# Chunk states of an SSD scan from three fp32r products of split operands, in place of one fp32 product

## The chip, the cores and the metric

The kernel is one program on one core of a Trainium2 chip. The metric is the device time of one execution in microseconds (us). Three executions of the kernel before took 2356.79, 2356.94 and 2358.75 us; the median is 2356.94 us. TensorE is called PE in the profile, VectorE DVE, ScalarE ACT, GpSimd POOL and SyncE SP.

## The reference

The reference is one layer of a hybrid encoder on 1024 tokens of width 1024: windowed attention beside a Mamba-2 style SSD scan, a merge, a cross-attention and an MLP. The change touches one line of the SSD scan, the state that each chunk of 128 tokens contributes:

```python
xdt = (x * dt[..., None]).reshape(b, c, CHUNK, G, r, P)
decay_states = jnp.exp(a_cs[..., -1:] - a_cs)
states = jnp.einsum('bcsgn,bcgrs,bcsgrp->bcgrpn', Bc, decay_states, xdt)
```

There are 8 groups (G), in each 4 heads of width 64 and a state of 128; 8 chunks; and two directions, forward and backward. So for each group and chunk a matrix B of 128 tokens by 128 state entries is multiplied with x, scaled by a coefficient of its token, head and direction: 128 tokens by 512 columns (two directions of 256). Chunk 0 needs only its forward half and chunk 7 only its backward half.

## The kernel before

All large products are made on PE with operands of the type fp32r. An operand is split into a high part (an ACT copy into an fp32r tile) and a low part (the fp32 value minus the high part, on POOL for weights, on DVE for activations), and three products are summed in PSUM: high by high, high by low, low by high. The helper `mm3` (its products stand at L85, L89 and L90) does this. Smaller products of the scan are single fp32 products.

The scan is `ssd_phase`. Eight groups go through it one after another. For a group four projections run as jobs (`conv_job` 0 and 1 make the two x tiles `cx`, 2 makes B as `cB`, 3 makes C as `cC`), then a `z_job`, whose products `zp` run while the states are computed. A job's weights are loaded one job ahead by `wload`: DMA into `raw`, ACT copy to `whi` (L66), POOL subtraction to `wlo` (L69). `conv_post` follows each conv job: one ACT operation (L379), four DVE operations from PSUM (L383, L385, twice each), an ACT tanh (L387) and a DVE operation (L388).

PE's order is that of the code (`manual_schedule`), and the table `jobs` sets after how many steps of a job another piece runs: in the z job `tm_b` after step 4, `state(q, c)` after step 8c + 8. The other engines' orders are made by a scheduler when the program is built; each engine then takes its instructions strictly in that order.

- `tm_b` turns B to token order: four PE transposes (L482) into one PSUM tile `tm`, an ACT copy (L483) into `btok`, twice.
- `state` scales x on DVE into `xs` (L502, 128x512, both directions always), makes one fp32 product of `btok` and `xs` into the PSUM tile `st` (L506) and adds the result to the running states `prev` (L509 to L514).
- `tm_x`, in job 3, turns the two `cx` tiles into `xtok`; after that the two `cx` buffers are free until the next group's job 0.
- `step` and `prep` make the outputs of a chunk; POOL's `p` (L572, x times the skip weight) belongs to `step`, and runs early since it needs only `xtok`.

The buffers that matter: `xs` has 2, `cx` has 2, the PSUM tag `p` (`tm`, `zp`, `st` and others) has 4.

Of the kernel before, what the change touches and what calls it, by code (L numbers as in the profile page):

```python
# [7 lines left out]
F32 = mybir.dt.float32  # L8
F32R = mybir.dt.float32r
I32 = mybir.dt.int32  # L10
AF = mybir.ActivationFunctionType
ALU = mybir.AluOpType
# [4 lines left out]
P = 128  # L17
S = 1024
D = 1024
NT = 8  # L20
# [395 lines left out]
def ssd_phase(kx, ins, dr):  # L416
# [3 lines left out]
    V, A, G, PE = nc.vector, nc.scalar, nc.gpsimd, nc.tensor  # L420
    with tc.tile_pool(name="p1", bufs=1) as sp, tc.manual_schedule(engines={mybir.EngineType.PE}):
        ca = kx.conv_pool
# [3 lines left out]
        def heads(ap):  # L426
            return ap.rearrange("p (h q) -> p h q", h=4)
# [46 lines left out]
                    V.scalar_tensor_tensor(zb, zb, 1.0, zp, ALU.add, ALU.mult)  # L474
            return load, run

        def tok_major(src, dst):
            for b in range(2):
                pt = kx.pp.tile([P, 512], F32, tag="p", name="tm")
                for j in range(4):  # L480
                    c = 4 * b + j
                    PE.transpose(pt[:, j * P:(j + 1) * P], src[:, c * P:(c + 1) * P], kx.ident)  # L482
                A.activation(dst[:, 4 * b:4 * b + 4], pt.rearrange("p (c j) -> p c j", c=4), AF.Copy)  # L483

        def tm_x(q):
            q.xtok = ca.tile([P, NT, 256], F32, tag="xtok", bufs=1, name="xtok")
            for i in range(2):
                tok_major(q.cx[i], q.xtok[:, :, i * P:(i + 1) * P])

        def tm_b(q):  # L490
            q.btok = ca.tile([P, NT, P], F32, tag="btok", bufs=1, name="btok")
            tok_major(q.BT, q.btok)
            q.prev = sp.tile([P, NT, 2, 256], F32, tag="prev", bufs=1, name="prev")

        def decay(q, d, c):
            o = 64 * d + 32 * (c // 4) + 4 * q.g
            return kx.dec[:, o:o + 4, c % 4:c % 4 + 1].broadcast_to([P, 4, 64])

        def state(q, c):
            prev = q.prev  # L500
            xs = sp.tile([P, 2, 4, 64], F32, tag="xs", bufs=2, name="xs")
            V.tensor_tensor(xs, heads(q.xtok[:, c]).unsqueeze(1).broadcast_to([P, 2, 4, 64]),  # L502
                            kx.coef[:, c // 4, c % 4, :, q.hs].unsqueeze(3).broadcast_to([P, 2, 4, 64]), ALU.mult)
            lo, hi = (256 if c == NT - 1 else 0), (256 if c == 0 else 512)
            st = kx.pp.tile([P, 512], F32, tag="p", name="st")
            PE.matmul(st[:, lo:hi], q.btok[:, c], xs.rearrange("p d h q -> p (d h q)")[:, lo:hi],  # L506
                      start=True, stop=True)
            if c == 0:
                A.activation(prev[:, 1, 0], st[:, :256], AF.Copy)  # L509
            elif c < NT - 1:  # L510
                V.tensor_tensor(heads(prev[:, c + 1, 0]), heads(prev[:, c, 0]), decay(q, 0, c), ALU.mult)
                V.tensor_tensor(prev[:, c + 1, 0], prev[:, c + 1, 0], st[:, :256], ALU.add)
            if c > 0:
                A.activation(prev[:, c - 1, 1], st[:, 256:], AF.Copy)  # L514
# [89 lines left out]
        for g in range(NG):  # L604
            q, o = gs[g], gs[g - 1]
            scan = lambda *cs: [(step, o, c) for c in cs] if g else []
            if g == 0:
                job(conv_job(q, 3), {8: [(tm_x, q)]})
            else:
                job(conv_job(q, 0), {8: [(step, o, 7)], 16: [(step, o, 6)]})  # L610
                job(conv_job(q, 1), {8: [(step, o, 5)], 16: [(step, o, 4)]})
                job(gate_job(g), {8: [(step, o, 3)], 16: [(step, o, 2)]})
                job(conv_job(q, 2), {8: [(step, o, 1)], 16: [(yt, o), (step, o, 0)]})
                job(conv_job(q, 3), {8: [(tm_x, q)], 16: [(yt, o)]})
            at = {8 * c + 8: [(state, q, c)] for c in range(NT)}
            at[4] = [(tm_b, q)]
            at[56] += [(prep, q, 7)]
            at[64] += [(prep, q, 6), (mask, q, 7)]
            job(z_job(q), at)
        q = gs[7]  # L620
# [1093 lines left out]
```

## Time and profile before

| | before |
|---|---|
| median of 3 runs | 2356.94 us |
| the profiled execution: its time, its span | 2356.88 us, 2355.1 us |
| granted PE clock | 0.999 of full speed |
| DVE, ACT, POOL busy, share of the span | 67%, 48%, 37% |
| fp32 state products, L506 | 64: 48 of 512 columns, 16 of 256 |

The span is what the trace covers; 1.8 us of the execution lie around it. Busy time of PE is modelled: matmuls are pipelined, so one row's duration overlaps the next, and the distance from one start to the next is what a product costs in a stream. Several engines work at the same time, so idle time of an engine matters only where another waits for it. The page's times are from the span's start. In a row of the timeline stand the start, the duration, engine, line, operation, output and input tiles, their shapes and the count of merged instructions; what stands in square brackets is the idle time ahead of it and its releaser. An fp32 product stands in the records as two matmul instructions.

### The profile page before, as it was taken

To read this page: it belongs to the slowest core of one execution; us is meant where nothing else is said; L and a number is where in the kernel's file an instruction comes from. 1 tells how busy PE (TensorE), PEld (TensorE's weight loads), DVE (VectorE), ACT (ScalarE), POOL (GpSimd) and SP (SyncE) were. 2 spreads that over 40 slices of the span, in tenths; PEclk is the share of its full clock that TensorE was granted. 3 is DMA by queue.
4 is the path that set the end of the run, shared out by engine and by line. 5 is a ranking of instruction groups with operands and counts; after the bars stand their busy time and mean duration, and the time that the engine had idled before them with its cause. 6 is when DMAs were issued, how large, how long until landed. Compare 5 with 4: busy or idle time off the path is not lost.

```text
span 2355.1 us, 32190 instructions
## 1 busy us (share of the span) xinstructions
PE 2323.0 (99%) x11812; PEld 1928.8 (82%) x11812; DVE 1570.3 (67%) x2523; ACT 1124.4 (48%) x2398; POOL 872.9 (37%) x827
## 2 busy tenths in 40 slices
PE   9999999999999999999999999999999999999998
PEld 7888888888888888877777888888988887788887
DVE  4766656576665654374668887975585456689984
ACT  4454545555454555486765442346453333134341
POOL 2344626354462634354540014215475444200010
PEclk9999999999999999999999999999999999999999
DMA  6322323233232322111126157202353345722301
GB/s 221 90 81 90 107 73 110 79 100 89 90 108 72 111 78 99 39 36 55 41 73 248 57 169 264 77 14 85 106 177 129 108 127 182 293 78 86 120 27 72
DMA packets 150033, 251.01 MB, mean 107 GB/s; under 512 B 11250, under 2 KB 86130, under 8 KB 149876
## 3 DMA queue, kind: packets, MB, share of 16 engines
q1 hardware_dynamic: 79264, 210.67, 26.3%
q10 hardware_dynamic: 70612, 38.29, 5.7%
q8 instruction: 93, 1.52, 0.3%
q14 instruction: 64, 0.52, 0.1%
HBM read 201.47 MB, written 47.45 MB: 106 GB/s over the span
## 4 chain that ended last, share of the span: by engine, by line
PE 80%; DVE 9%; ACT 4%; DMA 3%; issue 2%; POOL 1%; SPq 0%; ACTq 0%; POOLq 0%; DVEq 0%
PE dps L1484 10%; PE mps L1484 8%; PE pb L1279 6%; PE cps L90 5%; PE cps L85 4%; PE cps L89 4%; PE pc L1279 3%; PE zp L89 3%; PE zp L90 3%; PE zp L85 3%; PE cb L560 2%; PE yo L564 2%; PE st L506 2%; PE gps L85 2%; PE gps L89 2%
## 5 line engine op out<-in xcount | busy, mean ns | idle before, releaser
L69 POOL TENSOR_TENSOR wlo<-raw,whi 128x1024 fp32r<-128x1024 f32 x104 | 255.4, 2456 | 413.8 <-ACT whi L66 400.0
L1435 ACT ACTIVATE kt<-row 128x512 fp32r<-128x512 f32 x264 | 144.1, 620 | 186.5 <-PE dps L1484 83.3
L1484 PE MATMUL mps<-kt 128*128 128x512 f32 x1008 | 230.4, 390 | 1.5 <-DVE kt L1436 1.5
L1484 PE MATMUL dps<-kt 128*128 128x512 f32 x1008 | 228.6, 389 | 0.0
L1484 PEld LDWEIGHTS mps<-kt 128*128 128x128 f32 x1008 | 188.7, 188 | 42.0 <-DVE kt L1436 3.0
L1484 PEld LDWEIGHTS dps<-kt 128*128 128x128 f32 x1008 | 189.3, 188 | 39.2
L85 PE MATMUL cps<-kt,whi 128*128 128x512 f32 x512 | 215.1, 420 | 0.0
L66 ACT ACTIVATE whi<-raw 128x1024 fp32r<-128x1024 f32 x104 | 109.7, 1056 | 209.2 <-PE cps L89 43.4
L90 PE MATMUL cps<-kt,wlo 128*128 128x512 f32 x512 | 200.0, 391 | 0.0
L89 PE MATMUL cps<-kt,whi 128*128 128x512 f32 x512 | 199.3, 389 | 0.0
L1436 DVE TENSOR_TENSOR kt<-row,kt 128x512 fp32r<-128x512 f32 x264 | 172.1, 700 | 3.5 <-ACT kt L1435 3.4
L124 POOL TENSOR_TENSOR rr<-rv,mhalf 128x1 f32<-128x1 f32 (+1 forms) x50 | 35.0, 701 | 238.1 <-DVE rv L122 232.1
L528 POOL TENSOR_SCALAR_AFFINE_SELECT rows<-rows 128x512 f32<-128x512 f32 x64 | 42.7, 667 | 211.4 <-DMA rows<-d_cs 205.8
L1225 POOL TENSOR_TENSOR wop<-w,wop 128x512 fp32r<-128x512 f32 x64 | 86.4, 1352 | 86.8 <-ACT wop L1224 76.5
L89 PEld LDWEIGHTS cps<-kt,whi 128*128 128x128 f32 x512 | 96.3, 188 | 25.4 <-issue 6.7
L85 PEld LDWEIGHTS cps<-kt,whi 128*128 128x128 f32 x512 | 96.3, 188 | 25.0 <-issue 5.5
L90 PEld LDWEIGHTS cps<-kt,wlo 128*128 128x128 f32 x512 | 96.1, 188 | 20.7
L537 ACT ACTIVATE ef<-rows,ebias 128x128 f32<-128x128 f32 x256 | 90.3, 392 | 43.2 <-PE cb L560 43.2
L538 ACT ACTIVATE eb<-rows,ebias 128x128 f32<-128x128 f32 x256 | 89.0, 392 | 30.3 <-POOL rows L530 30.2
L85 PE MATMUL gps<-kt,whi 128*128 128x512 f32 x240 | 102.3, 426 | 0.0
L732 POOL TENSOR_SCALAR t<-t,den 128x384 f32<-128x384 f32 (+1 forms) x128 | 69.2, 559 | 80.2 <-DVE den L730 63.1
L721 DVE CUSTOM_DVE_ANT_0 t<-sps,bias 128x384 f32<-128x384 f32 (+1 forms) x128 | 64.4, 522 | 51.5 <-PE sps L720 49.5
(370 smaller groups left out, 6396.3 us busy)
## 6 DMA issues: line engine op xcount, KB each, us to landing
rows<-d_cs ACTq DMA_DIRECT2D x128, 256.0 KB, 3.9
raw<-in_wssd_dram SPq DMA_DIRECT2D x48, 512.0 KB, 3.6
raw<-in_wup_dram SPq DMA_DIRECT2D x40, 512.0 KB, 3.7
d_u<-c SPq DMA_DIRECT2D x64, 256.0 KB, 2.3
row<-in_wdn_dram SPq DMA_DIRECT2D x28, 512.0 KB, 6.1
row<-d_u SPq DMA_DIRECT2D x28, 512.0 KB, 6.6
x<-in_x_dram SPq DMA_DIRECT2D x16, 512.0 KB, 6.7
raw<-in_wg_dram SPq DMA_DIRECT2D x16, 512.0 KB, 3.5
```

Of the source, the lines that this page charges most:

```text
L66: steps = [nc.scalar.activation(hi, raw, AF.Copy)]
L69: steps.append((eng or nc.gpsimd).tensor_tensor(lo, raw, hi.bitcast(F32), ALU.subtract))
L85: i = mm(out, l[0], r[0], start=first, stop=False)
L89: mm(out, l[0], r[1], start=False, stop=False)
L90: mm(out, l[1], r[0], start=False, stop=last)
L537: A.activation(ef[:, h], rows[:, 0, h], AF.Exp, bias=kx.ebias[:, b, j, 0, o:o + 1])
L538: A.activation(eb[:, h], rows[:, 1, h], AF.Exp, bias=kx.ebias[:, b, j, 1, o:o + 1])
L1225: self.kx.nc.gpsimd.tensor_tensor(t[:, 1], src, t[:, 0].bitcast(F32), ALU.subtract)
L1279: self.kx.nc.tensor.matmul(ps, w[:, i, ks], act[:, k, j], start=start and k == 0 and m == 0, stop=k == 3 and m == 2, skip_group_check=True)
L1435: nc.scalar.activation(t[:, j, 0], src, AF.Copy)
L1436: nc.vector.tensor_tensor(t[:, j, 1], src, t[:, j, 0].bitcast(F32), ALU.subtract)
L1484: self.kx.nc.tensor.matmul(ps[t], lt[:, k, x, ts], rt[:, k, y], start=n in (1, 2, 5) and k == 0 and m == 0, stop=k == 3 and m == 2, skip_g ...
```

## The change

`tm_b` now makes two fp32r tiles, `bh` (ACT copy) and `bl` (DVE: PSUM minus `bh`), and puts them in the two `cx` buffers; `btok` is gone. `state` makes `xs` only for the directions that are needed (128x256 in chunks 0 and 7), copies it on ACT to `xh`, subtracts on POOL to `xl`, and sums three fp32r products: `bh` by `xh`, `bl` by `xh`, `bh` by `xl`. The tiles `xs`, `xh` and `xl` have two buffers each.

```diff
--- before.py
+++ after.py
@@ -474,13 +474,16 @@
                     V.scalar_tensor_tensor(zb, zb, 1.0, zp, ALU.add, ALU.mult)
             return load, run
 
-        def tok_major(src, dst):
+        def tok_major(src, dst, low=None):
             for b in range(2):
                 pt = kx.pp.tile([P, 512], F32, tag="p", name="tm")
                 for j in range(4):
                     c = 4 * b + j
                     PE.transpose(pt[:, j * P:(j + 1) * P], src[:, c * P:(c + 1) * P], kx.ident)
-                A.activation(dst[:, 4 * b:4 * b + 4], pt.rearrange("p (c j) -> p c j", c=4), AF.Copy)
+                cs, pc = slice(4 * b, 4 * b + 4), pt.rearrange("p (c j) -> p c j", c=4)
+                A.activation(dst[:, cs], pc, AF.Copy)
+                if low is not None:
+                    V.tensor_tensor(low[:, cs], pc, dst[:, cs].bitcast(F32), ALU.subtract)
 
         def tm_x(q):
             q.xtok = ca.tile([P, NT, 256], F32, tag="xtok", bufs=1, name="xtok")
@@ -488,8 +491,8 @@
                 tok_major(q.cx[i], q.xtok[:, :, i * P:(i + 1) * P])
 
         def tm_b(q):
-            q.btok = ca.tile([P, NT, P], F32, tag="btok", bufs=1, name="btok")
-            tok_major(q.BT, q.btok)
+            q.bhl = [ca.tile([P, NT, P], F32R, tag="cx", bufs=2, name=n) for n in ("bh", "bl")]
+            tok_major(q.BT, *q.bhl)
             q.prev = sp.tile([P, NT, 2, 256], F32, tag="prev", bufs=1, name="prev")
 
         def decay(q, d, c):
@@ -498,13 +501,22 @@
 
         def state(q, c):
             prev = q.prev
-            xs = sp.tile([P, 2, 4, 64], F32, tag="xs", bufs=2, name="xs")
-            V.tensor_tensor(xs, heads(q.xtok[:, c]).unsqueeze(1).broadcast_to([P, 2, 4, 64]),
-                            kx.coef[:, c // 4, c % 4, :, q.hs].unsqueeze(3).broadcast_to([P, 2, 4, 64]), ALU.mult)
+            xh = sp.tile([P, 512], F32R, tag="xh", bufs=2, name="xh")
+            xl = sp.tile([P, 512], F32R, tag="xl", bufs=2, name="xl")
             lo, hi = (256 if c == NT - 1 else 0), (256 if c == 0 else 512)
+            d0, d1 = lo // 256, hi // 256
+            xf = sp.tile([P, 512], F32, tag="xs", bufs=2, name="xs")
+            V.tensor_tensor(xf[:, lo:hi].rearrange("p (d h q) -> p d h q", h=4, q=64),
+                            heads(q.xtok[:, c]).unsqueeze(1).broadcast_to([P, d1 - d0, 4, 64]),
+                            kx.coef[:, c // 4, c % 4, d0:d1, q.hs].unsqueeze(3).broadcast_to([P, d1 - d0, 4, 64]),
+                            ALU.mult)
+            A.activation(xh[:, lo:hi], xf[:, lo:hi], AF.Copy)
+            G.tensor_tensor(xl[:, lo:hi], xf[:, lo:hi], xh[:, lo:hi].bitcast(F32), ALU.subtract)
             st = kx.pp.tile([P, 512], F32, tag="p", name="st")
-            PE.matmul(st[:, lo:hi], q.btok[:, c], xs.rearrange("p d h q -> p (d h q)")[:, lo:hi],
-                      start=True, stop=True)
+            bh, bl = (t[:, c] for t in q.bhl)
+            PE.matmul(st[:, lo:hi], bh, xh[:, lo:hi], start=True, stop=False)
+            PE.matmul(st[:, lo:hi], bl, xh[:, lo:hi], start=False, stop=False)
+            PE.matmul(st[:, lo:hi], bh, xl[:, lo:hi], start=False, stop=True)
             if c == 0:
                 A.activation(prev[:, 1, 0], st[:, :256], AF.Copy)
             elif c < NT - 1:
```

The scheduler's order of three engines, from the z job of the second group. Line numbers of the changed kernel are higher: its `xs` is at L509 (before L502), the conv lines keep theirs, and "waits" names the engines or DMA queues whose semaphore a row awaits. DVE before, from the last operation on `cB` on:

```order
L388 SCALAR_TENSOR_TENSOR cB<-th,cB 128x1024 [waits Activation_49]
L502 TENSOR_TENSOR xs<-xtok,coef 128x512 [waits Activation_49]
L502 TENSOR_TENSOR xs<-xtok,coef 128x512
L383 SCALAR_TENSOR_TENSOR cC<-cps,cols,cC 128x1023 [waits PE_49,Activation_49]
L385 SCALAR_TENSOR_TENSOR cC<-cps,cols,cC 128x1023 [waits DVE_49]
L511 TENSOR_TENSOR prev<-prev,dec 128x256 [waits Activation_49]
L383 SCALAR_TENSOR_TENSOR cC<-cps,cols,cC 128x1022 [waits DVE_49]
L502 TENSOR_TENSOR xs<-xtok,coef 128x512 [waits PE_49]
```

DVE in the changed kernel, from the same operation on:

```order
L388 SCALAR_TENSOR_TENSOR cB<-th,cB 128x1024 [waits Activation_49]
L509 TENSOR_TENSOR xs<-xtok,coef 128x256 [waits Activation_49]
L509 TENSOR_TENSOR xs<-xtok,coef 128x512
L509 TENSOR_TENSOR xs<-xtok,coef 128x512 [waits Pool_49] x2
L383 SCALAR_TENSOR_TENSOR cC<-cps,cols,cC 128x1023 [waits PE_49,Activation_49]
L486 TENSOR_TENSOR bl<-tm,bh 128x512 [waits Activation_49]
L385 SCALAR_TENSOR_TENSOR cC<-cps,cols,cC 128x1023 [waits DVE_49]
L486 TENSOR_TENSOR bl<-tm,bh 128x512 [waits Activation_49]
```

Four `xs` now stand ahead of the first operation on `cC` instead of two, and the third and fourth wait for POOL, since they reuse the buffers that `xl` of chunks 0 and 1 reads. The two `bl` stand behind the first and the second operation on `cC`.

POOL before, from the two early `p` of the same group on:

```order
L572 TENSOR_TENSOR p_2422<-xtok,dsk 128x256 [waits Activation_49,Pool_49]
L572 TENSOR_TENSOR p_2487<-xtok,dsk 128x256
L69 TENSOR_TENSOR wlo<-raw,whi 128x1024 [waits DMAHW2_49,PE_49,Activation_49]
L528 AFFINE_SELECT rows<-rows 128x512 [waits DMAHW1_49,Activation_49]
L530 AFFINE_SELECT rows<-rows 128x512 [waits DMAHW2_49]
L528 AFFINE_SELECT rows<-rows 128x512 [waits DMAHW3_49,Activation_49]
```

POOL in the changed kernel, from there on:

```order
L584 TENSOR_TENSOR p_2524<-xtok,dsk 128x256 [waits Activation_49,Pool_49]
L584 TENSOR_TENSOR p_2589<-xtok,dsk 128x256
L514 TENSOR_TENSOR xl<-xs,xh 128x256 [waits Activation_49]
L514 TENSOR_TENSOR xl<-xs,xh 128x512 [waits Activation_49]
L69 TENSOR_TENSOR wlo<-raw,whi 128x1024 [waits DMAHW2_49,PE_49,Activation_49]
L514 TENSOR_TENSOR xl<-xs,xh 128x512 [waits PE_49,Activation_49] x4
L514 TENSOR_TENSOR xl<-xs,xh 128x512 [waits DVE_49,PE_49,Activation_49]
L540 AFFINE_SELECT rows<-rows 128x512 [waits DMAHW1_49]
```

The first two `xl` stand ahead of the weight subtraction `wlo`, all others behind it, between it and the masking of `rows`.

PE before, around the group's first state product, which is chunk 0:

```order
L89 MATMUL zp<-wlo,kt 128x256
L90 MATMUL zp<-whi,kt 128x256
L506 MATMUL st<-xs,btok 128x256 [waits DVE_49,Activation_49]
L85 MATMUL zp<-z_1928,kt 128x256
L89 MATMUL zp<-z_1929,kt 128x256
L90 MATMUL zp<-z_1928,kt 128x256
```

PE in the changed kernel, at the same place:

```order
L89 MATMUL zp<-wlo,kt 128x256
L90 MATMUL zp<-whi,kt 128x256
L517 MATMUL st<-xh,bh 128x256 [waits Activation_49]
L518 MATMUL st<-xh,bl 128x256 [waits DVE_49]
L519 MATMUL st<-xl,bh 128x256 [waits Pool_49]
L85 MATMUL zp<-z_1979,kt 128x256
L89 MATMUL zp<-z_1980,kt 128x256
L90 MATMUL zp<-z_1979,kt 128x256
```

The second product waits for DVE (the first `bl`), the third for POOL (the first `xl`); behind them stand the rest of the `zp` products.

## Prediction

> **What bounds the kernel now.** I read the page's busy times first, then the stretch that the change touches in the view of stages, then that stretch row by row in the timeline of each engine.
>
> ```profile
> PE 2323.0 (99%) x11812; PEld 1928.8 (82%) x11812; DVE 1570.3 (67%) x2523; ACT 1124.4 (48%) x2398; POOL 872.9 (37%) x827
> 212.00:264.00 52.00, 52.00 (x333) 45.49 (x332) 27.33 (x42) 27.26 (x69) 17.83 (x21) 1.00 0.23 72
> ```
>
> The second row is the z job of group 1 (the second group): the stretch, its length, then PE, PEld, DVE, ACT and POOL busy, and PE's clock. PE is busy in all 52.00 us at full clock, the others in half or a third. So here whatever shortens PE's stream shortens the kernel, and whatever makes PE wait lengthens it, one for one; work on the other engines is free until PE waits for it. In the timeline of PE stand the state products:
>
> ```profile
> 222.74 0.28 PE L90 MATMUL zp<-whi,kt 128*128 128x256 f32 x1
> 222.86 0.60 PE L506 MATMUL st<-xs,btok 128*128 128x256 f32 x2
> 223.11 0.47 PE L85 MATMUL zp<-z,kt 128*128 128x256 f32 x1
> 223.41 0.29 PE L89 MATMUL zp<-z,kt 128*128 128x256 f32 x1
> ...
> 226.17 1.02 PE L506 MATMUL st<-xs,btok 128*128 128x512 f32 x2
> 226.63 0.68 PE L85 MATMUL zp<-z,kt 128*128 128x256 f32 x1
> 227.14 0.29 PE L89 MATMUL zp<-z,kt 128*128 128x256 f32 x1
> ```
>
> An fp32r product of 256 columns takes 0.12 us of the stream (222.74 to 222.86). From the start of `st` to the second `zp` behind it are one `st` and one such product. So the narrow `st` costs 0.55 - 0.12 = 0.43 us, the wide one 0.97 - 0.12 = 0.85.
>
> **What PE gains.** The price of a wide fp32r product is read from a conv job: between these rows lie 20 products, 4.56 us, so 0.228 each.
>
> ```profile
> 206.26 0.39 PE L85 MATMUL cps<-kt,whi 128*128 128x512 f32 x1
> 210.82 0.39 PE L90 MATMUL cps<-kt,wlo 128*128 128x512 f32 x1
> L506 PE MATMUL st<-xs,btok x128: 377/590/594, 119.9 to 866.8; 128*128 128x512 f32 x96, 128*128 128x256 f32 x32
> ```
>
> The last row counts two records for a product: 48 wide and 16 narrow. Removed: 48 x 0.85 + 16 x 0.43 = 47.7 us. Added: 144 x 0.228 + 48 x 0.12 = 38.6. **PE's stream gets 9.1 us shorter**, 1.14 in a group (six wide, two narrow). The extra weight loads are in the 0.228 and 0.12, since there each product has its own.
>
> Here the Trainium skill has another price. Its page "TensorE: Matmul & The Clock Gate", section "Back-to-back issue gap", gives N / 2.4 + 2.5 ns, for 512 columns 216 ns; by it a group's gain would be about 0.2 us larger. The stream above, at 228 ns, is the same operand type in this kernel, and decides.
>
> **What PE comes to wait for.** At the first state of a group the second product needs `bl`, and in DVE's order this stands behind four `xs` and the first operation on `cC`. The timelines of DVE, POOL and ACT at this place, before:
>
> ```profile
> 215.86 2.13 DVE L502 TENSOR_TENSOR xs<-xtok,coef 128x512 f32<-128x512 f32 x2
> 221.56 1.28 DVE L383 SCALAR_TENSOR_TENSOR cC<-cps,cols,cC 128x1023 f32<-128x1023 f32 x1 [3.58 <-ACT cC L379]
> 222.88 1.28 DVE L385 SCALAR_TENSOR_TENSOR cC<-cps,cols,cC 128x1023 f32<-128x1023 f32 x1
> 224.08 0.41 DVE L511 TENSOR_TENSOR prev<-prev,dec 128x256 f32<-128x256 f32 x1
> ```
>
> ```profile
> 215.80 0.62 POOL L572 TENSOR_TENSOR p<-xtok,dsk 128x256 f32<-128x256 f32 x1 [4.76 <-ACT xtok L483]
> 215.80 1.64 POOL L572 TENSOR_TENSOR p<-xtok,dsk 128x256 f32<-128x256 f32 x2 [4.76 <-ACT xtok L483]
> 219.36 2.38 POOL L69 TENSOR_TENSOR wlo<-raw,whi 128x1024 fp32r<-128x1024 f32 x1 [1.92 <-ACT whi L66]
> ```
>
> ```profile
> 218.23 1.06 ACT L66 ACTIVATE whi<-raw 128x1024 fp32r<-128x1024 f32 x1 [2.57 <-PE cps L89]
> 221.42 1.08 ACT L483 ACTIVATE btok<-tm 128x512 f32<-128x512 f32 x2
> ```
>
> Two operations `xs` took 2.13 us, though one alone takes 0.685 (median below), and the second `p` took longer than the first. DVE and POOL get in each other's way. The clearest case, and one that shows who goes first, in the timelines of POOL and DVE:
>
> ```profile
> 882.99 0.72 POOL L574 TENSOR_TENSOR p<-p,t 128x256 f32<-128x256 f32 x1
> 883.68 0.72 POOL L520 TENSOR_TENSOR prev<-prev,cb_t 128x256 f32<-128x256 f32 x1
> 903.88 2.40 POOL L69 TENSOR_TENSOR wlo<-raw,whi 128x1024 fp32r<-128x1024 f32 x1 [3.03 <-ACT whi L66]
> ```
>
> ```profile
> 883.74 0.94 DVE L580 TENSOR_TENSOR yz<-yz,p 128x256 f32<-128x256 f32 x1 [1.20 <-POOL p L574]
> 904.01 2.54 DVE L580 TENSOR_TENSOR yz<-yz,p 128x256 f32<-128x256 f32 x1
> ```
>
> An addition of two SBUF tiles that takes 0.41 us alone took 2.54, because `wlo` had started 0.13 earlier: it ended at 906.55, 0.27 after `wlo`, so it worked from 0.14 before the end of `wlo`. It was held for the whole instruction. And at 883.74 DVE was released by the end of a `p` (883.71), but POOL's next instruction had started at 883.68 and went first. Operations with one input in PSUM aren't held: L383 at 221.56 took 1.28 beside `wlo`.
>
> The Trainium skill says the same: "SBUF — State Buffer", section "Who interferes with whom", has a DVE instruction with two SBUF inputs contend with a GpSimd instruction that reads SBUF, on one read port, and the first holds it to its end. The rows at 904 agree (2.54 us). By the page's rule taken alone the change must be suspected wherever `xl` or `wlo` meets `xs`; without the rule the sum would be that of the first rival below.
>
> Prices of what is new, from the views of single lines (minimum, median, maximum in ns):
>
> ```profile
> L502 DVE TENSOR_TENSOR xs<-xtok,coef x64: 679/685/1122, 113.6 to 860.9; 128x512 f32<-128x512 f32 x64
> L511 DVE TENSOR_TENSOR prev<-prev,dec x48: 412/419/422, 122.6 to 861.5; 128x256 f32<-128x256 f32 x48
> L156 DVE TENSOR_TENSOR kt<-nt,kt x40: 673/682/695, 19.0 to 1698.0; 128x512 fp32r<-128x512 f32 x40
> L1225 POOL TENSOR_TENSOR wop<-w,wop x64: 1268/1294/2165, 1763.6 to 2015.9; 128x512 fp32r<-128x512 f32 x64
> L520 POOL TENSOR_TENSOR prev<-prev,cb_t x48: 719/740/1279, 149.8 to 897.4; 128x256 f32<-128x256 f32 x48
> ```
>
> `bl` is an operation like L156, 0.68 us. `xl` of 512 columns is like L1225, 1.28; of 256 columns like L520, 0.72. No row shows `xl` itself: from below half a `wlo`, 1.19, bounds it; from above the longest L1225, 2.17, which contains a wait. I take the undisturbed 1.28.
>
> Now the chain in groups 1 to 7, with the times of group 1. (1) The first `p` lets go at 216.29; the first `xs`, half as wide, works to 216.70, the second `p` to 217.18, the second `xs` from 217.05 to 217.74. (2) ACT has `xh` of chunk 0 (some 0.4 us; `btok`, twice as wide, took 1.08 for two) at 217.1; its `xl` gets the port at 217.61 and ends at 218.33. (3) This releases the third `xs`, 218.36 to 219.05. `xl` of chunk 1 gets the port behind it, 218.92 to 220.20. (4) ACT's `whi` (218.23, now behind `xh` of chunk 1, some 0.1 later) is done at 219.4, so `wlo` follows `xl` at once, at 220.16, to 222.55. (5) The fourth `xs` is released at 220.23, 0.07 too late, as at 883.74; it works from 222.42 to 223.10. (6) L383 on `cC`, at 221.56 before, starts at 223.02, and 1.20 later (as 222.88 to 224.08) `bl`: 224.22 to 224.90. (7) PE has made the first product at 222.86, wants the second at 222.98 and gets it at 224.96. **The stall is 1.98 us**, 0.84 more than the group's gain. It does not matter in (3) whether `xl` or `xs` goes first: `wlo` is ready at 219.4 either way and `xs` of chunk 3 waits for an `xl` that ends later.
>
> Group 0 has less room before `cC`:
>
> ```profile
> 115.42 2.10 POOL L572 TENSOR_TENSOR p<-xtok,dsk 128x256 f32<-128x256 f32 x2 [0.63 <-ACT xtok L483]
> 117.48 2.39 POOL L69 TENSOR_TENSOR wlo<-raw,whi 128x1024 fp32r<-128x1024 f32 x1
> 118.32 1.28 DVE L383 SCALAR_TENSOR_TENSOR cC<-cps,cols,cC 128x1023 f32<-128x1023 f32 x1 [1.85 <-ACT cC L379]
> 119.85 0.60 PE L506 MATMUL st<-xs,btok 128*128 128x256 f32 x2
> ```
>
> The two `p` end at 117.25 (the narrow `xs` ahead of them gives 0.27). `xl` to 117.91, `xl` to 119.14, third `xs` to 119.70 (held, then first at the port), `wlo` to 121.95, fourth `xs` to 122.50, L383, `bl` to 124.31. PE wants it at 119.97 and gets it at 124.37: a stall of 4.40.
>
> **What stays hidden.** ACT's 64 `xh` (0.54 each, as `btok`), POOL's `xl` and DVE's `bl` fill idle time: a state comes every 3.3 us or more (222.86 to 226.17), and after the first stall each `xh` and `xl` of a chunk is ready 2 to 6 us ahead (chunk 2: `xl` ends about 227.2, its product comes at 231.6). Were that cover gone, each 0.1 us in the 56 later states would cost 5.6. The `tm` banks are let go by the second `bl` at 226.6, ahead of chunk 2's product, which waits for it. `cx` of the next group is written after a conv job of 48 products, 10.9 us, when all state products are done. SP's queue is unchanged; ACT issues one load of `rows` behind an `xh`, and POOL masks it that much later, for a `step` of the next group's jobs.
>
> **The sum:** -9.1 + 7 x 1.98 + 4.40 = +9.2 us on the profiled execution's 2356.88, which is 0.06 below the median shown: **2366.1 us**, 0.39% slower. With `xl` between its bounds 1.19 and 1.53 (a fifth above what I take; 2.17 would hold a second wait) the eight stalls shift by -0.7 to +2, and with steps of 0.1 us in the rest this case has 2362 to 2371.
>
> **The rivals.**
> *The fourth `xs` gets the port before `wlo`* (POOL slower to begin its next instruction than DVE to be released). For it: the margin is 0.07 us. Against it: 883.74. Then in groups 1 to 7 L383 stays at 221.56, `bl` ends at 223.44, the stall is 0.52; group 0, where `wlo` queues earlier, keeps 4.40: -9.1 + 3.6 + 4.4 = -1.1, **2355.8 us**. Chance 0.16.
> *The gain arrives whole* (faster): PE doesn't wait, since `bl` comes in time; 2356.88 - 9.1 = **2347.8 us**. It decides itself at 222.98: `bl` must end before. Against it, L383 ahead of it in DVE's order cannot start before 221.56, so 223.44 is the earliest; only an order other than shown would do it. Chance 0.06, with cases in which the stalls stay under 4.4 us in all.
> *More than the first state waits*: `xh` waits on ACT behind tanh and exponentials, `xl` on POOL behind masks. At 0.15 us a state it adds 8.4, **2374 us**. Against it, the margins above. Chance 0.07.
> *It doesn't do what it says*: three fp32r products cost PE what one fp32 product did. Then the stalls stand alone, +18.3, **2375 us**. The streams above speak against it. Chance 0.03.
>
> **How the numbers follow.** My forecast has 0.68, the rivals 0.16, 0.06, 0.07 and 0.03. The range 2355 to 2372 takes in the forecast's own and the first rival, about 0.84. Faster or slower by 0.2% (4.7 us, about what a measurement of this kernel can tell from no change) means below 2352.2 or above 2361.6. Faster: the whole gain, 0.06. Same: the first rival and the lower edge of my case, 0.2. Slower: the rest, 0.74.
>
> **What would show it.** In the changed kernel's trace: wide states at 0.68 us of PE's stream; PE idle at the second product of the first state, about 2 us in seven groups and 4 in the first, released by `bl`; one `xs` of some 2.9 us on DVE beside `wlo`, ahead of a late L383. Were that `xs` short, the first rival holds; were PE idle at other states, the third does; were PE never idle, I am wrong about DVE's order.

## The result and the profile after

The changed kernel takes 2380.75 us (median of 5 runs, 2376.66 to 2383.52) against 2356.94 for the kernel before: 1.0096 times as long, 95% interval 1.0081 to 1.011. The forecast was 2366.1 with a range up to 2372. The sign was right, the size 15 us too small. The profiled execution took 2381.32 us, its span is 2379.5.

First the page's busy times and, from the view of stages, the z job of group 1 (the stretch, its length, busy time of PE, PEld, DVE, ACT and POOL, PE's granted clock, DMA):

```profile
PE 2326.0 (98%) x11876; PEld 1946.9 (82%) x11876; DVE 1617.0 (68%) x2539; ACT 1156.0 (49%) x2462; POOL 950.0 (40%) x891
216.00:268.00 52.00, 50.20 (x331) 46.38 (x329) 31.88 (x43) 30.57 (x75) 24.80 (x25) 0.97 0.24 70
```

In the kernel before, this job had PE busy in all 52.00 us at clock 1.00. Now PE is idle for 1.80 us of it, and the clock is 0.97. The busy time doesn't show what the second costs: a product that runs slowly counts as busy. The longest of PE's waits in the whole trace (total, how often, the longest):

```profile
PE st L518 <- DVE bl L486: 16.5, 8, 4.0
```

That is the forecast's wait at the forecast's place: once in each group, at the second product of the first state, longest in group 0. PE's timeline there in group 1 (start, duration, line, tiles; in brackets the idle time and its releaser):

```profile
227.54 0.28 PE L517 MATMUL st<-xh,bh 128*128 128x256 f32 x1
229.62 0.39 PE L518 MATMUL st<-xh,bl 128*128 128x256 f32 x1 [1.80 <-DVE bl L486]
229.84 0.29 PE L519 MATMUL st<-xl,bh 128*128 128x256 f32 x1
...
230.80 0.28 PE L89 MATMUL zp<-z,kt 128*128 128x256 f32 x1
230.91 0.35 PE L90 MATMUL zp<-z,kt 128*128 128x256 f32 x1
231.06 0.41 PE L85 MATMUL zp<-z,kt 128*128 128x256 f32 x1
231.27 0.42 PE L89 MATMUL zp<-z,kt 128*128 128x256 f32 x1
```

From 227.54 to 229.62 instead of 0.12: a stall of 1.96 us. Then something that was not forecast: 1.3 us later, at about 230.95, the distance from one `zp` to the next grows from 0.12 to 0.21 us, though nothing is waited for. And the chain behind the stall, on DVE and POOL:

```profile
223.04 0.69 DVE L509 TENSOR_TENSOR xs<-xtok,coef 128x512 f32<-128x512 f32 x1 [0.64 <-POOL xl L514]
224.91 2.87 DVE L509 TENSOR_TENSOR xs<-xtok,coef 128x512 f32<-128x512 f32 x1 [1.18 <-POOL xl L514]
227.69 1.27 DVE L383 SCALAR_TENSOR_TENSOR cC<-cps,cols,cC 128x1023 f32<-128x1023 f32 x1
228.89 0.67 DVE L486 TENSOR_TENSOR bl<-tm,bh 128x512 fp32r<-128x512 f32 x1
```

```profile
221.91 2.96 POOL L514 TENSOR_TENSOR xl<-xs,xh 128x256 fp32r<-128x256 f32 x2
224.84 2.38 POOL L69 TENSOR_TENSOR wlo<-raw,whi 128x1024 fp32r<-128x1024 f32 x1
```

The fourth `xs`, released by `xl`, starts 0.07 us after `wlo` and is held until `wlo` ends at 227.22; L383 and `bl` follow it.

To see the slow stretch, the view of stages is cut at the times at which the clock changes. The starts of these stretches lie whole multiples of 3.413 us apart (from 230.98 to 439.20 are 61, from there to 545.01 are 31), so the cuts are such a grid:

```profile
227.57:230.98 3.41, 1.61 (x14) 1.41 (x13) 3.41 (x5) 0.91 (x2) 0.23 (x1) 1.00 0.46 154
230.98:234.40 3.42, 3.42 (x18) 3.42 (x18) 3.09 (x4) 0.00 (x0) 1.05 (x1) 0.50 0.00 0
234.40:237.81 3.41, 3.41 (x28) 3.28 (x27) 2.59 (x4) 2.34 (x4) 1.29 (x1) 1.00 0.00 0
333.38:336.80 3.42, 1.82 (x15) 1.82 (x16) 3.42 (x5) 0.90 (x2) 0.68 (x1) 1.00 0.45 158
336.80:340.21 3.41, 3.41 (x28) 3.28 (x28) 3.41 (x5) 1.82 (x3) 1.24 (x2) 1.00 0.00 0
435.78:439.20 3.42, 1.64 (x14) 1.44 (x14) 3.42 (x4) 0.69 (x2) 0.67 (x1) 1.00 0.55 181
439.20:442.61 3.41, 3.41 (x19) 3.41 (x18) 3.41 (x5) 0.90 (x2) 1.28 (x1) 0.50 0.01 5
```

In the first window PE is busy for 1.61 of 3.41 us, so idle for 1.80. In the second the granted clock is 0.50, for the whole window and no longer. Group 2 shows the other case: its stall falls across two windows, 1.60 us of it in this one, and the clock stays at 1.00. A window at half clock does 16 products in the time of 28: 16 x 0.213 = 3.41 us for what takes 16 x 0.12 = 1.92. It costs **1.5 us**. Groups 1, 3, 4, 5 and 7 have one such window, group 0, with the long stall, has two; groups 2 and 6 have none. The period, from a group's last `st` product to that of the next, says the same: 103.0 us before, 105.3 to 105.4 with such a window, 103.9 without.

### The profile page after: what moved, and what is told of

Same layout as the page of the kernel before. It is cut to its first block, busy times and chain, and to the rows that moved or that the text cites. A ratio compares the mean times of both kernels' runs of the same rounds, so it can differ in the third digit from the quotient of the medians.

```text
span 2379.5 us, 32503 instructions
## 1 busy us (share of the span) xinstructions
PE 2326.0 (98%) x11876; PEld 1946.9 (82%) x11876; DVE 1617.0 (68%) x2539; ACT 1156.0 (49%) x2462; POOL 950.0 (40%) x891
## 4 chain that ended last, share of the span: by engine, by line
PE 76%; DVE 11%; ACT 4%; issue 3%; DMA 3%; POOL 2%; SPq 0%; ACTq 0%; POOLq 0%; DVEq 0%
PE dps L1496 10%; PE mps L1496 8%; PE pb L1291 5%; PE cps L90 4%; PE cps L85 4%; PE cps L89 4%; PE pc L1291 3%; PE zp L85 2%; PE zp L89 2%; PE zp L90 2%; PE cb L572 2%; PE yo L576 2%; PE gps L85 2%; PE gps L89 2%; PE gps L90 2%
## 5 line engine op out<-in xcount | busy, mean ns | idle before, releaser
L514 POOL TENSOR_TENSOR xl<-xs,xh 128x512 fp32r<-128x512 f32 (+1 forms) x64 | 81.6, 1276 | 112.6 <-ACT xh L513 111.2
L1176 POOL TENSOR_TENSOR wd<-row,wd 128x1024 fp32r<-128x1024 f32 x4 | 11.2, 2799 | 228.4 <-ACT wd L1175 228.4
```

## The experiments

Three theories stood at the start. A: the stall comes from the `xs` ahead of L383, as forecast, and the half clock comes from the stall. B: the slow stretch has another cause, such as the new operands. C: `bl` is late for another reason. Each result is given with its ratio to the kernel before in the same series. "The states' phase" is from the first `zp` product (group 0) to the last `st` product (group 7): 750.7 us before, 769.6 in the changed kernel.

### The kernels again

Both kernels were run once more, without an edit.

> The changed kernel as it is, once more. From the first product of the attention to the last of the program it took 1437.7 us in its first trace and the kernel before 1431.3; the code there is the same. Theory A (these 6.4 us vary from one execution to the next, whatever the kernel): another value between 1430 and 1439 us in this trace, off the first by 2 us or more, while the states' phase repeats within 2 us. Theory B (the change costs about 6 us there): 1436 to 1439 us again, and in the repeat of the kernel before 1430 to 1433.

> The kernel before, once more, as a measure of how far one trace of it differs from another. Theory A: from the first product of the attention to the last of the program 1428 to 1438 us, off the 1431.3 of its first trace by 2 us or more. Theory B: 1430 to 1433 us. Both: no wait of PE at st, periods of 103.0 us, the clock at 1.00 through the groups.

The changed kernel took 2379.38 us (1.0091, 1.0077 to 1.0104), the kernel before 2358.81 (1.0006, 0.9996 to 1.0016). The states' phase repeats: 770.1 and 750.7 us. The half clock fell on five of the groups 1 to 7 again, but on others (2, 3, 4, 6 and 7): the grid lies otherwise against the program. From the first product of the attention (`kps`) to the first of the last stage (`dps`, whose 315.3 us are the same everywhere), in the views of these tiles (count, durations, first and last start), changed kernel, first trace:

```profile
L85 PE MATMUL kps<-kt,whi x32: 387/390/579, 933.7 to 1108.2; 128*128 128x512 f32 x32
L85 PE MATMUL dps<-kt x64: 389/389/392, 2056.1 to 2099.0; 128*128 128x512 f32 x64
```

and in the repeat:

```profile
L85 PE MATMUL kps<-kt,whi x32: 387/389/579, 934.2 to 1108.8; 128*128 128x512 f32 x32
L85 PE MATMUL dps<-kt x64: 389/389/392, 2050.5 to 2093.4; 128*128 128x512 f32 x64
```

That is 1122.4 and 1116.3 us for the same code and the same kernel. The two traces of the kernel before have 1116.0 and 1113.9. So of the 24.4 us by which the span grew, 6.4 arose in code that doesn't differ, and a repeat has 0.3 of them. The expectation for theory A holds in both runs: these times vary from one execution to the next. Whether the change adds something there on average, two traces of each kernel can't tell; this is taken up at the end. The waits that differ most between the first trace and the repeat lie in the merge: 1.6 us for a `wlo` whose weights landed late, 2.4 for `kt`; the repeat has 0 and 0.6.

### Work in place of the wait

Ahead of the first product of each group's first state stand n products whose result nothing reads. They go into the half of `st` that chunk 0 doesn't use.

```diff
+            if c == 0:
+                for i in range(16):
+                    l, r = act_pair(kx.hT[0], i % NK)
+                    PE.matmul(st[:, 256:], l[:, :P], r[:, :256], start=True, stop=True)
             PE.matmul(st[:, lo:hi], bh, xh[:, lo:hi], start=True, stop=False)
```

> Edit: ahead of the first product of each group's first state stand 16 products of 256 columns (0.12 us each, 1.92 us in all) into the half of st that chunk 0 doesn't use and nothing reads; PE works through the time in which it waited, and L518 starts no later. Theory A (the idle time itself lowers the granted clock): the clock stays at 1.00 in the z jobs of groups 1 to 7, the 1.5 us lost behind the stall in six groups go, the group's period falls from 105.38 to about 103.9 us, and the time is 2367 to 2372 us. Theory B (the slow stretch comes from the work around the states, not from the idle time): the period stays at 105.4 in six groups and the time at 2378 to 2383 us; if the products only add to the wait, 2393 us.

> Edit: as the run with 16 products, with 8 of them (0.96 us), so that a wait of about 1.0 us is left in groups 1 to 7 and about 3.2 us in group 0. Theory A1 (a wait has to be longer than about 1 us to lower the clock): the clock stays at 1.00 in groups 1 to 7, and the time is 2367 to 2373 us. Theory A2 (any wait of 1 us lowers it): a stretch at 0.50 in most groups, 2377 to 2382 us. Theory B (the idle time has no part in it): 2378 to 2383 us, with the slow stretches where they were.

> Edit: as the runs with 16 and 8 products, with 4 of them (0.48 us), so that a wait of about 1.45 us is left in groups 1 to 7 and some 3.7 us in group 0. So far a wait of 1.0 us left the clock at 1.00 in seven groups, and waits of 1.8 to 1.96 us lowered it in six groups of seven or eight. Theory A1 (the clock falls where PE idles for half or more of a stretch of 3.41 us on a fixed grid, that is 1.7 us): 1.00 in groups 1 to 7, periods of 103.9 us, time 2367 to 2375 us. Theory A2 (the bound lies between 1.0 and 1.45 us): periods of 105.4 us in most groups, time 2376 to 2383 us.

| products | wait left, group 1 | half-clock windows, groups 1 to 7 | period | states' phase | time | ratio |
|---|---|---|---|---|---|---|
| 0 (changed kernel) | 1.80 | 5 | 103.9 or 105.4 | 769.6 | 2380.75 | 1.0096 (1.0081 to 1.011) |
| 4 | 1.32 | 0 | 103.9 | 762.8 | 2369.59 | 1.0051 (1.0037 to 1.0066) |
| 8 | 0.84 | 0 | 103.9 | 762.0 | 2371.93 | 1.0054 (1.0037 to 1.0071) |
| 16 | none | 0 | 103.9 | 761.6 | 2368.54 | 1.0042 (1.0027 to 1.0057) |

Idle time replaced by useless work makes the kernel faster: by 9 to 12 us in the median, of which the states' phase shows 6.8 to 8.0. With 16 products the stages of group 1 read:

```profile
227.00:232.00 5.00, 5.00 (x45) 4.92 (x43) 4.74 (x4) 2.59 (x4) 2.57 (x2) 1.00 0.53 178
232.00:237.00 5.00, 5.00 (x40) 4.87 (x40) 5.00 (x7) 1.40 (x3) 1.30 (x1) 1.00 0.08 32
```

The products end when `bl` comes, so PE reaches the rest no sooner than with the wait; only the half clock is gone. Theory B is out. Theory A1 of the runs with 8 and with 4 products holds too: a wait of 0.84 or 1.32 us is still there in groups 1 to 7, and the clock is not touched. In group 0, where more wait is left, it still falls (8 products; first two rows group 1, last two group 0):

```profile
229.79:233.20 3.41, 2.57 (x22) 2.37 (x21) 3.41 (x4) 0.90 (x2) 0.46 (x1) 1.00 0.45 154
233.20:236.61 3.41, 3.41 (x28) 3.28 (x28) 3.41 (x6) 1.59 (x3) 1.23 (x2) 1.00 0.00 0
...
123.97:127.39 3.42, 1.16 (x9) 1.16 (x10) 3.42 (x5) 0.74 (x2) 0.03 (x1) 1.00 0.46 153
127.39:130.80 3.41, 3.41 (x18) 3.41 (x17) 3.29 (x4) 0.17 (x1) 1.27 (x1) 0.50 0.03 7
```

Idle 0.84 us: nothing follows. Idle 2.26 us: a window at 0.50.

### The third and fourth `xs` held back

```diff
+            with tc.issue_after(q.lowb.ins) if c > 1 else ExitStack():
                 V.tensor_tensor(xf[:, lo:hi].rearrange("p (d h q) -> p d h q", h=4, q=64),
...
```

Here `q.lowb` is the second `bl` of the group; what stands in the block is queued behind it on DVE.

> Edit: VectorE issues the products xs of chunks 2 to 7 only behind the second bl of their group; nothing else is changed. Theory A (the stall of about 1.9 us at the second product of the first state comes from the third and fourth xs, which wait for POOL's xl ahead of L383 on cC; and the clock that is granted at 0.50 for about 3.4 us behind it comes from that stall): L383 on cC starts about 2 us earlier against the PE, the stall falls from 17.8 us in sum to under 4, the clock stays at 1.00 in the z jobs, and the time is 2348 to 2353 us. Theory B (the stall is one for one, and the slow products behind it come from something else, such as the extra reads of bh, bl, xh and xl): the stalls go, the slow stretches of about 1.5 us in six groups stay: 2358 to 2363 us. Theory C (bl is late for another reason than the xs ahead of L383, for instance the transposes or the copy bh): stalls and time stay near those of the changed kernel, 2378 to 2383 us.

2384.83 us (1.0107, 1.0092 to 1.0122): slower than any of the three theories had it, and the reason is none of the three. PE's waits in the states' phase:

```profile
PE st L521 <- POOL xl L516: 14.4, 8, 1.8
PE st L520 <- DVE bl L486: 2.9, 7, 0.4
```

The wait for `bl` has gone from 16.5 to 2.9 us, and L383 started 1.24 us ahead of the first state instead of 0.15 behind it (227.69 against 227.54 above). In the timelines of DVE and PE, group 1:

```profile
222.83 1.28 DVE L383 SCALAR_TENSOR_TENSOR cC<-cps,cols,cC 128x1023 f32<-128x1023 f32 x1 [3.90 <-PE tm L482]
224.07 0.28 PE L519 MATMUL st<-xh,bh 128*128 128x256 f32 x1
```

So theory C is out, the `xs` ahead of L383 were the cause. But the third `xs` now came so late that its `xl` was missing at the third state, 1.8 us in each group, and the half clock followed this wait as it had followed the other, in six of eight groups:

```profile
231.07:234.48 3.41, 1.60 (x11) 1.13 (x10) 1.74 (x3) 0.97 (x2) 3.00 (x2) 1.00 0.00 0
234.48:237.90 3.42, 3.42 (x19) 3.42 (x18) 2.20 (x5) 1.01 (x2) 2.03 (x2) 0.50 0.02 5
```

Another product, another engine that is waited for, the same half clock: so it hangs on PE's idle time, whatever PE waits for.

### Only the fourth `xs` on held back

The same edit with `c > 2`.

> Edit: only the products xs from the fourth on (chunks 3 to 7) stand behind the second bl; the third keeps its place, and the states theirs (step 8 on). With the third and fourth held, L383 on cC started 1.24 us ahead of the first state instead of 0.15 us behind it and the wait for bl fell to 0.41 us, but the third state then waited 1.8 us for its xl. Theory A (the fourth xs alone, which waits for POOL's second xl and then shares the port with wlo, makes bl late): in groups 1 to 7 the wait at L518 stays at 0.4 to 0.5 us, none at L519, the clock at 1.00, the period at 102.2 to 102.4 us, and the time is 2350 to 2356 us. Theory B (the third xs has a share of its own, since it waits for the first xl): a wait of 1.0 to 1.5 us at L518, no fall of the clock, periods of 103 to 103.4 us, 2357 to 2361 us. Rival (the wait moves to the fourth state's xl): 1.8 us at L519 with a stretch at half clock, 2370 us and above.

In the trace theory A holds for groups 1 to 7. Group 0 waits 1.2 us, the others 0.41; there is no wait for `xl` and no half clock in this phase:

```profile
PE st L520 <- DVE bl L486: 4.1, 8, 1.2
```

So in groups 1 to 7 the fourth `xs` alone made `bl` late; the third, in its old place, costs nothing there (0.41 us with it held and with it not). In group 0 the third has a share of its own: the wait is 1.2 us here and was 0.1 with both held. The period is 102.5 us (102.2 to 102.4 expected), the states' phase 747.5 us, 3.2 shorter than before. The time did not follow: 2358.67 us (1.0004, 0.9996 to 1.0013), above the 2350 to 2356 expected. Its trace lost time in the merge and the cross-attention, but one trace doesn't explain the median of 11 executions. This is a miss, and its cause is open.

### The first state later

```diff
-            at = {8 * c + 8: [(state, q, c)] for c in range(NT)}
+            at = {8 * c + 8 if c else 14: [(state, q, c)] for c in range(NT)}
```

> Edit: the first state of each group stands behind step 14 of the z job instead of step 8, 6 steps or 2.2 us of products later; the chain of xs, L383 and bl is untouched. Theory A (the stall is bl that comes 1.9 us after PE wants it, and the low clock follows from it): in groups 1 to 7 the stall goes or stays under 0.3 us, in group 0 it falls from 4.2 to about 2 us; the clock stays at 1.00 but for group 0; time 2348 to 2354 us. Theory B (the slow stretches have another cause): 2358 to 2364 us. Rival (the wait moves to the second state at step 16, whose prev or xl is late now): 2365 us and above, with a wait named at L517 or L519.

2356.63 us (0.9994, 0.9984 to 1.0003): 24 us faster than the changed kernel, yet above the expectation. The waits and the clock are as expected: PE does `zp` products while `bl` is made, the period is 101.86 us in every group, and the one wait is that of group 0, with one half-clock window behind it:

```profile
PE st L518 <- DVE bl L486: 2.1, 1, 2.1
```

The states' phase takes 745.5 us, 5.2 less than before. The median is 1.8 us better.

### Group 0 later still

The first three states of group 0 behind steps 20, 23 and 27, those of the other groups as above.

> Edit: in group 0 the first three states stand behind steps 20, 23 and 27 of the z job instead of 8, 16 and 24, in the other groups the first stands behind 14. In the run with all first states at step 14 the period of groups 1 to 7 was 101.86 us (103.0 before), and only group 0 still waited 2.1 us and had a stretch at half clock behind it. Theory A (stall and low clock were all that the change cost in this phase): no wait of PE at st, the clock at 1.00 up to the attention, the last st product about 8.5 to 9 us earlier than before, and the time 2347 to 2352 us. Theory B (the later phases take several us more with this change whatever its stalls): the states' phase gains 8.5 to 9 us and the time is still 2353 to 2357 us. Rival (in group 0 the third state now waits for xl, since the first three stand closer together): a wait at L519 of 0.5 to 1.5 us in group 0, time 2349 to 2354 us.

2355.97 us (0.9991, 0.998 to 1.0002), no better, and the expectation is missed: the time lies in theory B's range, but the states' phase took 748.2 us, a gain of 2.5 and not of 8.5 to 9. The wait in group 0 moved, as in the rival, but not to `xl`: it came at a PSUM buffer and at the first product of a state.

```profile
PE zp L85 <- ACT prev L526: 2.2, 1, 2.2
PE st L517 <- DVE zs L474: 0.8, 1, 0.8
PE yo L576 <- DVE t L580: 0.4, 1, 0.4
PE st L517 <- DVE bl L486: 0.4, 1, 0.4
```

States that stand closer together need their `st` banks read sooner: the third `zp` tile waited 2.2 us until a copy to `prev` had let a bank go. Half clock followed once more.

### Both edits

First in all groups: `c > 2` held, and the first state behind step 14.

> Edit: as the run with the fourth xs on held, and each group's first state behind step 14 of the z job instead of 8. Theory A (nothing but the wait for bl and the clock behind it stands against the gain in products): no wait at st in groups 1 to 7 nor, since bl comes earlier there too, more than 0.5 us in group 0; clock 1.00 up to the attention; periods of 101.86 us; from the first zp product to the last st product some 9 us less than the 750.4 us of before; time 2347 to 2352 us against about 2357. Theory B (group 0 has another wait, for prev or zs, as when its states stood closer together): 2350 to 2355 us.

2354.9 us (0.9987, 0.9978 to 0.9996), where theory A had 2347 to 2352. The time lies in theory B's range, but for a reason that neither theory had. Group 0 waits for nothing: 28.6 us from its first `zp` to its last `st` product, 29.7 before. In the other groups holding back does harm once it is no longer needed:

```profile
PE st L521 <- POOL xl L516: 4.0, 7, 0.6
```

0.6 us in seven groups, too short for the clock: periods of 102.6 us, and a states' phase of 746.9. (The kernel before has 750.7 there, not the 750.4 of the expectation.) So the last run holds back in group 0 alone.

```diff
+            with tc.issue_after(q.lowb.ins) if q.g == 0 and c > 2 else ExitStack():
                 V.tensor_tensor(xf[:, lo:hi].rearrange("p (d h q) -> p d h q", h=4, q=64),
...
+            at = {8 * c + 8 if c else 14: [(state, q, c)] for c in range(NT)}
```

> Edit: every group's first state behind step 14 of the z job, and the fourth xs and later ones behind the second bl in group 0 alone. With the first state at step 14 and nothing held the period of groups 1 to 7 was 101.86 us; with the fourth xs held as well group 0 had no wait and took 28.6 us from its first zp product to its last st product (29.7 before), while the held xs cost the other groups 0.6 us at L519. Theory A (both add up): no wait of PE at st in any group, clock 1.00 up to the attention, 28.6 us in group 0 and seven periods of 101.86 us, so 741.6 us from the first zp product to the last st product (750.7 before), and a time 9 us under the kernel before if the later phases take what they took there: 2347 to 2351 us. Theory B (the later phases give back some 4 us whatever the states do): the same 741.6 us, and 2351 to 2355 us.

**2353.58 us (0.9968, 0.9957 to 0.998): faster than both kernels.** PE waits at no `st` in any group. Its state products, first and last start:

```profile
L519 PE MATMUL st<-xh,bh x64: 280/393/393, 122.0 to 857.4; 128*128 128x512 f32 x48, 128*128 128x256 f32 x16
L520 PE MATMUL st<-xh,bl x64: 279/396/396, 122.1 to 857.5; 128*128 128x512 f32 x48, 128*128 128x256 f32 x16
L521 PE MATMUL st<-xl,bh x64: 274/404/404, 122.2 to 857.6; 128*128 128x512 f32 x48, 128*128 128x256 f32 x16
```

None is longer than 0.41 us, where the changed kernel had 0.58. With the first `zp` at 116.1 the states' phase takes 741.5 us (741.6 expected), 9.2 less than before. The median is 6.1 us below that of the kernel before in its series, so theory B of the last expectation fits the time: some 3 us are given back later, within what later phases vary by.

## Why the prediction missed

**The gain of PE's stream was right.** Forecast: 9.1 us, 1.14 in a group. In the last run, where nothing waits, the period is 101.86 us against 103.0, and the phase 9.2 us shorter.

**The chain behind the stall was right, step by step.** The third and fourth `xs` waited for `xl`; `wlo` started right behind the second `xl` and held the fourth `xs` (2.87 us, forecast "some 2.9"); L383 and `bl` came behind it; PE stalled at the second product of the first state and nowhere else. The sizes: 1.96 us in group 1 (forecast 1.98), 4.20 in group 0 (4.40), 17.8 in all (18.3). With the fourth `xs` behind `bl` the stall fell to 0.57 us, 0.41 of it idle (the first rival, in which the fourth `xs` doesn't hold up L383 either, had 0.52).

**The step that failed is in the first paragraph: "whatever makes PE wait lengthens it, one for one".** A stall of 1.9 us cost 1.9 us and, in most groups, a window of 3.41 us at half clock behind it, another 1.5. Measured behind the first state in the changed kernel: 2.05 us in group 0, 1.42 to 1.49 in five others, nothing in groups 2 and 6, 9.4 in all. The states' phase then follows: -9.1 + 17.8 + 9.4 = +18.1, measured +18.9. Most of the 0.8 left over lies between the second product and the third: they start 0.22 us apart (0.38 in group 0) and not 0.12. The forecast had +9.2. That the wait is the cause is shown by the three runs with work in its place, which took away the half clock of groups 1 to 7 and with it 6.8 to 8.0 us of the states' phase, and by the run in which the wait moved to another product and the half clock with it.

The trace of before could have warned. In the MLP's up stage, behind a wait of 2.3 us at `pb`, it has this (view of stages, kernel before, cut on the grid):

```profile
1761.87:1765.29 3.42, 1.33 (x6) 0.75 (x4) 1.92 (x4) 2.48 (x5) 1.71 (x2) 1.00 0.41 153
1765.29:1768.70 3.41, 3.17 (x8) 2.49 (x9) 3.41 (x3) 1.34 (x3) 3.41 (x3) 0.50 0.31 85
```

The mean clock of 0.999 hid it, and the forecast looked at the clock of the z job alone.

**The later phases were taken as fixed.** They vary by execution: from the first `kps` to the first `dps` the thirteen traces, whose code there is the same, span 1114 to 1124 us. In part these are half-clock windows that the same rule puts into the merge, cross-attention and up stages, in part weights that land late. Of the 14.7 us of miss, 9.4 are the clock in the states' phase; about 5 lie in the later phases, and their cause is open. Whether the change itself raises these, or the first trace only had a bad draw, is not settled: the repeat had 0.3 us there, but the medians of the changed and edited kernels lie between 1 us below and 5 us above what their states' phase gives, ten of eleven of them above. One wait differs steadily. In the cross-attention PE waits at `xsp` for `xq`, which ACT makes behind a weight load: 0.85 and 0.93 us in the two traces of the kernel before, 1.30 to 1.70 in ten of the eleven others, with a half-clock window behind it in seven. Every engine's order of instructions is the same there, and no run shows why the wait is longer.

**The rivals.** The whole gain (2347.8) did not come by itself, but an order that lets `bl` be in time gives it: 9.1 / 2356.9 is 0.39%, the last run has 0.32% (0.20 to 0.43). That more than the first state waits did not happen in the changed kernel, though the margin was small: held a little longer, the third state's `xl` was 1.8 us late. Three fp32r products do not cost what one fp32 product did.

## What to carry to other kernels

Where PE is the bound, a wait of PE has two prices: its length, and, where about 1.7 us or more of it fall into one window of 3.41 us, mostly a window at half clock behind it (1.5 us here, on a stall of 1.95); price it so, and look at the granted clock in windows of a few us, not at its mean. Cheaper products gain only if their operands are there: before a step is moved to other engines, ask which instruction stands last ahead of the first new operand in each engine's order, and give the consumer that much more distance. When an edit takes a wait away by holding something back, look for the next consumer of what is held.

## What the runs showed of the hardware

PE's granted clock is set window by window, on a grid of 3.41 us. A half-clock window follows one in which PE was idle for about half of the time or more. In the thirteen traces, cut this way from end to end, a window at full clock with at most 1.6 us idle never had one behind it (0.84 us in the run with 8 products, seven times). Between 1.65 and 1.85 us it came in 23 of 37 cases (after 1.80 us in group 1 of the changed kernel, not after 1.72 in its group 6). Above that it came in 19 of 20: in the run with 4 products a wait of 2.45 us in the up stage, 1.93 of it in one window, had none behind it. A window that is itself at half clock needs less: with 0.71 us idle or more in it the next was at half clock again (5 cases), with 0.56 or less at full clock. PE's ends are modelled, so these idle times are not exact. Since the grid lies otherwise in each execution, the same stall costs 1.9 us in one run and 3.4 in the next, and which groups pay changes from trace to trace.

The Trainium skill, "TensorE: Matmul & The Clock Gate", section "What's actually happening", has this window: 4096 cycles or 3413 ns, free-running. The traces agree, with starts whole multiples of 3.413 us apart. The Trainium skill, same page, section "HAM oscillation — how this bites in real kernels", has idle gaps of more than about 3.4 us as the danger. Here the traces differ: gaps of 1.8 us lowered the clock, and the measurement decides.
